# A 90-degree rotation of 96 images on one core: the first 1 MB load is made as two transfers of 4 KB pieces

## The chip, the cores and the metric

The kernel runs on one core of one Trainium2 chip. The metric is the device time of one execution in microseconds (us), taken as the median over several runs; lower is better. In what follows 1 MB of a load or store means 1024 KB, as the program counts it; rates in GB/s are in units of 10^9 bytes.

## The reference

Ninety-six images of 256 x 256 float32 values (a batch of 32 with 3 channels) are each turned by a quarter. Nothing is calculated on the values: every output value is an input value at another place.

```python
def setup_inputs():
    batch, c, h, w = 32, 3, 256, 256
    return {"x": np.random.randn(batch, c, h, w).astype(np.float32)}

def reference(x: np.ndarray) -> np.ndarray:
    return np.rot90(x, k=-1, axes=(-2, -1)).astype(np.float32)
```

25.17 million bytes have to be read from HBM and as many written.

## The kernel before

The input is seen as 24,576 rows of 256 values (1 KB each). They are cut into four groups, with the sizes 2, 2, 4 and 4 in units of 128 x 16 rows, that is 4, 4, 8 and 8 MB. Each group has its own tile in SBUF, `u0` to `u3` (`groups`, lines 41 to 44; the profile leaves the number out and shows `u`), and no tile is used twice, so that no load ever waits for space. Within a tile the rotation is done in place, by VectorE (DVE), which transposes blocks and reverses their order (`turn`, line 84), and by ScalarE (ACT), which copies pieces that had to step aside (`copy`, line 87). Spare room for these pieces is in two PSUM tiles (`spare0`, `spare1`) and two SBUF tiles (`extra`, `most`). The order of the DVE and ACT instructions is the order in which they are written; `keep` (line 75) fixes it.

**Loads.** All transfers are issued by the sync engine (SP), on one queue, in the order of the program. There are 15 loads. Group 0 is loaded in three of them: line 58, run twice, loads the two halves of slot 0 (`home[0]`), each 1 MB in 128 pieces (one for each partition) of 8 KB, and line 59 loads slot 1 (`home[1]`) with 2 MB, in 256 pieces of 8 KB. A piece of 8 KB is eight rows that lie side by side in HBM, and the 128 pieces of one load of line 58 lie side by side as well. Groups 1 to 3 are loaded by line 71 with 2 MB at a time, but the last 2 MB of group 3 are split in three (lines 67, 68 and 69: 0.5, 0.5 and 1 MB).

**Work.** The first DVE instruction (`turn_slab(u[:, 0], spare)`) reads both halves of slot 0, so it waits for both loads of line 58. Group 0 and group 1 follow as they land. The first instruction on group 2 reads pieces of all four of its loads, and from there DVE goes through groups 2 and 3.

**Stores.** There are ten, all behind the loads on the same SP queue. The first (line 178) waits in addition for the load of line 67 (`mark`), so that stores start when only the last 1.5 MB of loads are still under way. Groups 1 and 2 are stored by line 194, and group 3 by lines 190, 191, 192 and 194. Line 190 stores 64 pieces of 6 KB, line 191 stores 3 MB as soon as DVE and ACT are done with group 3, line 192 stores 64 pieces of 10 KB, and line 194 the last 4 MB.

**Semaphores of the transfers.** The transfers take eight semaphores in turn. So the issue of the ninth transfer, and of each one after it, has a wait for the transfer eight places before it, if that wait isn't already implied.

Of the kernel before, what the change touches and what calls it, by code (L numbers as in the profile page):

```python
# [9 lines left out]
def kernel(  # L10
# [14 lines left out]
    nc = tc.nc  # L25
# [6 lines left out]
    Q = E // 2  # L32
# [18 lines left out]
    def rows_of(rows, n):  # L51
        return rows[first[n] * P * R : (first[n] + sizes[n]) * P * R]


    ld = rows_of(rows_in, 0).rearrange("(s i p r) w -> s i p (r w)", s=2, i=2, p=P)
    home = [groups[0][:, s].rearrange("p (i f) -> p i f", i=2) for s in range(2)]
    for i in range(2):
        nc.sync.dma_start(out=home[0][:, i], in_=ld[1, i])  # L58
    nc.sync.dma_start(out=home[1], in_=ld[0].transpose([1, 0, 2]))  # L59
    for n in range(1, len(sizes)):  # L60
        I = sizes[n]
        ld = rows_of(rows_in, n).rearrange("(a i m r) w -> i m a (r w)", a=2, i=I, m=P // I)
# [162 lines left out]
```

## Time and profile before

| | us |
|---|---|
| median of 3 runs | 122.66 (122.62 to 122.70) |
| the profiled execution's own time | 122.64 |
| its span, first to last instruction | 120.8 |
| DVE busy, 25 instructions | 86.5 |
| ACT busy, 20 instructions | 29.0 |
| stores and loads together, 25 transfers | 97.6% of 16 DMA engines' span |

The time is 1.84 us more than the span; this part lies around the profiled instructions. The profile shows a transfer in two ways. Its issue is an instruction of the sync engine's sequencer (SPq), with a start and a duration. Its data move later, as packets on 16 DMA engines; a count of packets includes one very small packet for each transfer and engine, which tells the semaphore that this engine's part is done (25 transfers x 16 = 400 of them). "DMA share" in a table of windows is the time of the packets that start in the window, over 16 engines and the window's length; in short windows it can be over 1, since a packet counts where it starts.

### The profile page before, as it was taken

The page shows a single profiled execution, that of the slowest core. Times are in us where ns is not written, and L with a number is a line of the kernel's source. Part 1 is how long each engine was busy: PE and PEld are TensorE (multiplying, and loading weights), DVE is VectorE, ACT ScalarE, POOL GpSimd, SP SyncE. Part 2 cuts the span into 40 slices and gives each one's busy share as a digit, 9 for nine tenths or more (in the row PEclk, how much of TensorE's full clock was granted, in tenths as well). Part 3 has the DMA queues.
Part 4 walks back from the last instruction along what each step waited for, and adds up shares of the span by engine and source line. Part 5 has one row for each costly group of instructions (what it writes and reads, how often), then busy time and mean ns, then how long its engine had stood idle before and what let it go on. Part 6 is the DMA issues. An engine that isn't in the chain of part 4 may idle for free.

```text
span 120.8 us, 137 instructions
## 1 busy us (share of the span) xinstructions
DVE 86.5 (72%) x25; ACT 29.0 (24%) x20; POOL 0.2 (0%) x4
## 2 busy tenths in 40 slices
DVE  0039999999994099999999999999999990000000
ACT  0000400380005199508552296000003210000000
POOL 0000000000000000000000000000000000000000
DMA  2999999998989898989999999999999999999994
GB/s 87 431 434 423 447 434 434 434 521 347 521 347 521 347 521 347 510 358 412 456 407 418 423 428 434 418 434 434 423 434 434 434 434 456 401 423 456 434 434 174
DMA packets 3312, 50.33 MB, mean 417 GB/s; under 512 B 400, under 2 KB 400, under 8 KB 464
## 3 DMA queue, kind: packets, MB, share of 16 engines
q1 hardware_dynamic: 3312, 50.33, 97.6%
HBM read 25.17 MB, written 25.17 MB: 416 GB/s over the span
## 4 chain that ended last, share of the span: by engine, by line
DVE 44%; DMA 30%; SPq 4%; issue 3%; DVEq 0%
DVE u L84 34%; DMA u<-in_x_dram 30%; DVE spare L84 6%; DVE most L84 3%; SPq L71 3%; DVE extra L84 2%; SPq L58 1%; SPq L59 0%; DVEq L84 0%
## 5 line engine op out<-in xcount | busy, mean ns | idle before, releaser
L84 DVE STREAM_TRANSPOSE u<-u 128x2048 f32<-128x2048 f32 x16 | 59.6, 3792 | 0.3
L84 DVE STREAM_TRANSPOSE spare<-u 128x2048 f32<-128x2048 f32 (+1 forms) x4 | 11.8, 2982 | 12.6 <-DMA u<-in_x_dram 12.6
L87 ACT COPY u<-spare 128x512 f32<-128x512 f32 (+2 forms) x8 | 10.3, 1332 | 18.5 <-DVE u L84 13.7
L87 ACT COPY u<-extra 128x1024 f32<-128x1024 f32 (+1 forms) x3 | 5.7, 1938 | 11.1 <-DVE u L84 11.1
L87 ACT COPY u<-most 128x448 f32<-128x448 f32 x4 | 2.1, 563 | 20.4 <-DVE u L84 20.4
L87 ACT COPY spare<-u 128x1024 f32<-128x1024 f32 (+1 forms) x3 | 5.7, 1893 | 2.7 <-DMA u<-in_x_dram 2.7
L87 ACT COPY extra<-u 128x2048 f32<-128x2048 f32 x1 | 4.2, 4237 | 2.5 <-issue 2.5
L87 ACT ACT_TABLE_LOAD x1 | 1.3, 1283 | 13.0 <-DMA u<-in_x_dram 13.0
L84 DVE STREAM_TRANSPOSE extra<-u 128x2048 f32<-128x2048 f32 x1 | 3.9, 3898 | 0.0
L84 DVE STREAM_TRANSPOSE u<-spare 128x2048 f32<-128x2048 f32 x1 | 3.6, 3608 | 0.0
L84 DVE STREAM_TRANSPOSE most<-u 128x1792 f32<-128x1792 f32 x1 | 3.6, 3584 | 0.0
L84 DVE STREAM_TRANSPOSE spare<-spare 128x2048 f32<-128x2048 f32 x1 | 2.3, 2336 | 0.0
L84 DVE STREAM_TRANSPOSE extra<-extra 128x2048 f32<-128x2048 f32 x1 | 2.3, 2311 | 0.0
L209 POOL MEMSET const-uint8-127<- 128x1 uint8 x1 | 0.1, 102 | 0.0
L209 POOL MEMSET const-bfloat16-1.0<- 128x1 bf16 x1 | 0.1, 101 | 0.0
L209 POOL MEMSET const-float32-0.0<- 128x1 f32 x1 | 0.1, 98 | 0.2 <-issue 0.2
L209 POOL MEMSET const-float32-1.0<- 128x1 f32 x1 | 0.1, 98 | 0.0
## 6 DMA issues: line engine op xcount, KB each, us to landing
u<-in_x_dram SPq DMA_DIRECT2D x10, 2048.0 KB, 30.3
out_dram<-u SPq DMA_DIRECT2D x3, 4096.0 KB, 19.2
out_dram<-u SPq DMA_DIRECT2D x4, 2048.0 KB, 14.6
u<-in_x_dram SPq DMA_DIRECT2D x3, 1024.0 KB, 6.8
out_dram<-u SPq DMA_DIRECT2D x1, 3072.0 KB, 9.2
u<-in_x_dram SPq DMA_DIRECT2D x2, 512.0 KB, 33.4
out_dram<-u SPq DMA_DIRECT2D x1, 640.0 KB, 10.1
out_dram<-u SPq DMA_DIRECT2D x1, 384.0 KB, 5.6
```

Of the source, the lines that this page charges most:

```text
L58: nc.sync.dma_start(out=home[0][:, i], in_=ld[1, i])
L71: nc.sync.dma_start(out=to[i::I], in_=ld[i])
L84: keep(nc.vector.transpose(out=out, in_=in_))
L87: keep(nc.scalar.copy(out=out, in_=in_))
L209: nc = _bacc.Bacc("TRN2", target_bir_lowering=False, num_devices=1)
```

## The change

The first load of line 58, 1 MB in 128 pieces of 8 KB, becomes two transfers. Each covers all 128 partitions; the first moves the first 4 KB of each piece of 8 KB and the second the other 4 KB. Within one of these transfers the 4 KB pieces lie 8 KB apart in HBM. The second load of line 58 is unchanged, and so is all that follows, but all line numbers behind it grow by two.

```diff
-    for i in range(2):
-        nc.sync.dma_start(out=home[0][:, i], in_=ld[1, i])
+    tip = Q // 2
+    for f in (slice(0, tip), slice(tip, Q)):
+        nc.sync.dma_start(out=home[0][:, 0, f], in_=ld[1, 0][:, f])
+    nc.sync.dma_start(out=home[0][:, 1], in_=ld[1, 1])
     nc.sync.dma_start(out=home[1], in_=ld[0].transpose([1, 0, 2]))
```

`Q` is 2048 values, so `tip` is 1024 values, or 4 KB. In the program as it is built there are then 26 transfers, 16 of them loads. The semaphores are still taken in turn, so each transfer behind the first has the semaphore after the one that it had. For the waits of SP this comes to: the third load of group 2, which waited for no semaphore, now waits for the first 4 KB transfer; the fourth, which waited for the 1 MB transfer, waits for the second 4 KB transfer; every later load and every store waits for the same transfers as before. The first DVE instruction waits for three transfers in place of two. The instructions of DVE, ACT and GpSimd and their order are the same.

## The prediction

> **What bounds the kernel now.** I read the page first, for the share of each resource. DVE is busy for 72% of the span and ACT for 24%; the transfers are the resource that hardly ever rests.
>
> ```profile
> span 120.8 us, 137 instructions
> DMA  2999999998989898989999999999999999999994
> DMA packets 3312, 50.33 MB, mean 417 GB/s; under 512 B 400, under 2 KB 400, under 8 KB 464
> q1 hardware_dynamic: 3312, 50.33, 97.6%
> ```
>
> One digit is 3.02 us. The DMA row is full from the second slice to the last but one, and 97.6% of the span is 117.9 us, which is the stretch from the first packet to the last. So the end is the start of the data, plus the time of all packets, and idle time in between is near nothing. The change touches the first slice (the 2) and the number of packets.
>
> Second, the chain that ended last, in order of time, for how the start reaches the end (lines are left out):
>
> ```profile
> 0.73 0.37 SPq L58
> ...
> 1.16 0.42 SPq L58
> ...
> 5.53 36.61 DMA u<-in_x_dram
> ...
> 42.22 4.23 DVE spare L84
> ...
> 95.80 3.61 DVE u L84
> ```
>
> The loads stream until the fourth load of group 2 lands at 42.14; from there DVE works without a pause to 99.41, and line 191's store is issued at 99.47. What shifts the stream at its head shifts the landing at 42.14 by the same amount, and so DVE's chain too.
>
> Third, windows, for the head of the stream and for the place where both chains meet again. Columns: window and its length, busy time of DVE, ACT and GpSimd, clock, DMA share, GB/s.
>
> ```profile
> 1.00:1.70 0.70, 0.00 (x0) 0.00 (x0) 0.00 (x0) 1.00 0.00 0
> 1.70:2.50 0.80, 0.00 (x0) 0.00 (x0) 0.00 (x0) 1.00 0.73 164
> 2.50:2.70 0.20, 0.00 (x0) 0.00 (x0) 0.00 (x0) 1.00 0.00 0
> 1.70:4.85 3.15, 0.00 (x0) 0.00 (x0) 0.00 (x0) 1.00 0.87 333
> 4.85:7.25 2.40, 0.00 (x0) 0.00 (x0) 0.00 (x0) 1.00 1.03 434
> 99.85:100.70 0.85, 0.00 (x0) 0.00 (x0) 0.00 (x0) 1.00 0.99 412
> 100.70:101.00 0.30, 0.00 (x0) 0.00 (x0) 0.00 (x0) 1.00 2.17 915
> 101.00:101.35 0.35, 0.00 (x0) 0.00 (x0) 0.00 (x0) 1.00 0.00 0
> ```
>
> The first MB (128 packets, 1.70 to 4.85) takes 3.15 us and the second some 2.42. The difference, 0.73 us, I call the ramp: 16 first packets start between 1.70 and 2.50, one for each engine, then none until 2.70, so each first packet lasts long (0.73 x 0.80 us = 0.59 us on average). After 4.85 there is no second ramp, though another transfer begins there. At the other end, the packets of line 191 start together between 100.70 and 101.00 (915 GB/s is 16 packets of 16 KB, one for each engine, and two of 6 KB, then none): the queue had just run empty when this store came. So DVE's chain and the transfers are both at the limit there, and an edit would have to move both. One at the head does.
>
> Fourth, packet prices, from windows whose packets have one size: 7.8 to 9.8 (8 KB), 23 to 26 (32 KB) and 99.85 to 100.70 (6 KB, with 12 tiny ones).
>
> ```profile
> DMA packets 101, 0.83 MB, mean 414 GB/s; under 512 B 0, under 2 KB 0, under 8 KB 0
> q1 hardware_dynamic: 101, 0.83, 97.7%
> ...
> DMA packets 48, 1.57 MB, mean 524 GB/s; under 512 B 0, under 2 KB 0, under 8 KB 0
> q1 hardware_dynamic: 48, 1.57, 121.6%
> ...
> DMA packets 69, 0.35 MB, mean 412 GB/s; under 512 B 12, under 2 KB 12, under 8 KB 69
> q1 hardware_dynamic: 69, 0.35, 98.9%
> ```
>
> Share x 16 x window / packets gives 0.977 x 16 x 2.0 / 101 = 0.3095 us for 8 KB, 1.216 us for 32 KB, and 0.236 us for 6 KB (0.989 x 16 x 0.85 / 57, the tiny ones counted as nothing). Between 8 and 32 KB a KB costs 0.0378 us; that leaves 0.007 us per packet that doesn't depend on size. The same line gives 0.234 for 6 KB, so the measured 6 KB packet is within 0.002 us of it.
>
> **The change, step by step.**
>
> *Packets.* Of the first MB, each engine had 8 packets of 8 KB; it gets 16 of 4 KB. No 4 KB packet is in the trace. From below it can't cost less than half of 8 KB, 0.155 us (sum +0). From above I take the 6 KB packet, 0.236 us: 16 x 0.236 - 8 x 0.3095 = +1.30 us. The line gives 0.158, and the 6 KB row lies on that line, so I take 0.158: 16 x 0.158 - 8 x 0.3095 = +0.05 us. One more tiny packet per engine is at most the 0.002 x 57 / 12 = 0.01 us by which the 6 KB window is over the line. Together +0.06 us on every engine, and as no engine rests before 100.7, nothing hides it.
>
> The Trainium skill, "DMA: Bandwidth & Descriptors", in the warning on iDMA beside HBM reads, tabulates a load stream with 4 KiB rows alone at 408.7 GB/s. By it the first MB would need 2.57 us where the second now takes 2.42, and the sum would be +0.15 in place of +0.06 us; the trace has no such stream to compare.
>
> *Issue.* SP gets one more issue. The two of line 58 took 0.37 and 0.42 us, the one of line 59 with 256 pieces 0.43; the new ones have 128 pieces, so 0.4 us each, and 0.05 between. Only the first issue lies on the path, and it begins at 0.73 as before; from the spread of these rows its length may differ by 0.06 us either way. I take 0. All issues behind it come 0.45 us later. They are covered by data already queued: before, the second transfer was issued at 1.16 and its data began at 4.85. Now the first transfer alone holds 8 x 0.158 = 1.3 us of work behind its ramp, until about 3.6; the second transfer's packets, by the first's delay from issue to last start (0.73 to 2.50, 1.8 us), are there by about 2.95. Cover 0.65 us; without it, the shortfall would be paid one to one.
>
> *Waits on SP.* The third load of group 2 now waits for the first 4 KB transfer. Its turn comes at 4.88 + 0.45 = 5.3; that transfer's data end near 3.8 and land, with the 0.55 us by which the first MB landed behind its last packets (0.73 + 4.7 = 5.43 against 4.85 to 4.90), at 4.35. The wait is 0. The fourth load waits for the second 4 KB transfer, which lands near 5.5; its turn is at 5.9, where it waited before until 5.48. In both cases what stands behind on SP is later loads, with 8 MB and more queued ahead, some 20 us of cover. The other waits, those of all stores among them, are for the same transfers, and move with the stream.
>
> *DVE and ACT.* The first DVE instruction needs the second MB, which lands 0.06 later; DVE rests again for 4.53 us before 42.22, so this is lost in that gap. Landing at 42.14, DVE's end and line 191 all move by +0.06. So do the 16 engines.
>
> *The ramp.* 0.73 us at the head, and the only place where halving a piece could gain. If it all went: -0.73. If it were paid a second time by the second transfer: +0.73. The 16 engines each start one first packet between 1.70 and 2.50 and all start a second between 2.70 and 3.00; engines that began 0.7 us apart end together, so they wait for something that doesn't depend on how long each one's packet is. I take 0.
>
> Sum: +0.05 + 0.01 + 0 + 0 = +0.06, on the execution's own 122.64: 122.70 us. The median of the runs is 0.02 above that execution, so I forecast 122.72.
>
> **Rivals.**
>
> *The ramp shrinks (faster).* If a first packet's long time goes with its size, the first round is over sooner and the stream runs at full rate earlier. For it: the first packets last 0.59 us where later ones take 0.31, and they are the ones that get smaller. Against it: they end together whatever their start. If half the ramp goes: -0.37 + 0.06 = -0.31, 122.35 us. DVE's chain, hung on 42.14, would give it all on. The Trainium skill, "Perfetto Trace Analysis", under DMA optimizations, says that splitting may let some transfers start sooner, if the engines are generally idle; here they are idle only at the head, which this trace shows.
>
> *4 KB reads are slower than the line (slower).* Place: the 256 data packets of the first MB, read 8 KB apart. For it: nothing under 8 KB is ever loaded in this trace; the 6 KB row is a store. Against it: that row is on the line. Halfway between the two, 0.197 us a packet, the sum is 16 x 0.197 - 8 x 0.3095 + 0.01 = +0.69: 123.35 us. It decides (over 0.245 us) from 0.169 us a packet.
>
> *The ramp is paid twice (slower).* If the second transfer, now close behind, starts up on its own: +0.73 + 0.06, 123.45 us. Against it: no ramp at 4.85, where a transfer follows another. The Trainium skill, "DMA: Bandwidth & Descriptors", under rules for kernel authors, asks for 1 MiB or more per transfer, and its anatomy of a transfer gives a fixed cost of about 2.0 us (for transfers issued by GpSimd); taken as not overlapped that would be 124.7 us, and the seam at 4.85 disagrees.
>
> *It does nothing for the reader.* No instruction waits for a half alone: DVE waits for all three transfers. So an earlier half has no taker, and this rival ends where the forecast does.
>
> **How the numbers follow.** What a measurement of this kernel can tell from no change is about 0.2%, 0.245 us. The forecast has 0.50, with a range of its own of 122.55 to 122.90; the shrinking ramp 0.20 (122.1 to 122.4); slow 4 KB reads 0.20 (122.95 to 124.0); the second ramp 0.10. The forecast lies wholly within 0.2%, so the chances are 0.20, 0.50 and 0.30. The range 122.30 to 123.30 leaves out about 0.06 below and 0.14 above.
>
> **What would show it.** In the changed profile: packets go up by 128 + 16 to 3456; windows of 4 KB packets alone give 0.158 us each; the first MB ends 3.2 us after its first packet, with first packets still starting near 1.7; the wait at 42.14 ends at about 42.2 and line 191 is issued at about 99.53. A first round that is over before 2.7 would show the first rival, over 0.169 us per packet the second, and a stretch without packets near 3.6 the third. The forecast is wrong if the load of group 2 lands more than 0.2 us off 42.2, or if DVE's stretch of 57.3 us from there changes its length.

## The result and the profile after

The changed kernel takes 123.43 us (median of 6 runs, 123.40 to 124.08) against 122.64 for the kernel before (6 runs, 122.62 to 122.70). It is slower by 0.79 us. The ratio over all runs is 1.0073, with a 95% interval of 1.0059 to 1.0087; the two medians alone give 1.0064. The profiled execution took 123.48 us with a span of 121.7.

The page of the changed kernel, the rows that answer to those of before:

```profile
span 121.7 us, 138 instructions
DMA  3999999999999999999999999999999999999994
DMA packets 3456, 50.33 MB, mean 414 GB/s; under 512 B 416, under 2 KB 416, under 8 KB 736
q1 hardware_dynamic: 3456, 50.33, 97.4%
```

The packets are those that were counted beforehand, 128 + 16 more. The engines are nearly as full as before (97.4%). Summed over the trace, the packets take 118.5 us of an engine's time on average, where they took 118.0. So 0.5 of the 0.9 us of span is in the packets; the rest is time in which some engines wait, as shown below.

The chain that ended last, in order of time (start, length, what):

```profile
0.73 0.37 SPq L59
...
1.16 5.25 DMA u<-in_x_dram
...
6.42 36.66 DMA u<-in_x_dram
...
43.26 4.10 DVE spare L86
...
96.32 3.60 DVE u L86
```

The second 4 KB transfer lands at 6.41, where 5.5 was expected, and the fourth load of group 2 at 6.42 + 36.66 = 43.08 in place of 42.14: +0.94. The whole loss is there before DVE's long stretch begins.

Windows of the changed kernel's head (window, length, busy of DVE, ACT and GpSimd, clock, DMA share, GB/s), in the first four lines those of before, then two that separate the two 4 KB transfers:

```profile
1.70:2.50 0.80, 0.00 (x0) 0.00 (x0) 0.00 (x0) 1.00 0.69 189
2.50:2.70 0.20, 0.00 (x0) 0.00 (x0) 0.00 (x0) 1.00 0.91 307
1.70:4.85 3.15, 0.00 (x0) 0.00 (x0) 0.00 (x0) 1.00 0.87 263
4.85:7.25 2.40, 0.00 (x0) 0.00 (x0) 0.00 (x0) 1.00 1.01 420
...
2.50:3.90 1.40, 0.00 (x0) 0.00 (x0) 0.00 (x0) 1.00 0.93 231
4.43:5.15 0.72, 0.00 (x0) 0.00 (x0) 0.00 (x0) 1.00 0.97 398
```

and the kernel before in those last two:

```profile
2.50:3.90 1.40, 0.00 (x0) 0.00 (x0) 0.00 (x0) 1.00 0.89 374
4.43:5.15 0.72, 0.00 (x0) 0.00 (x0) 0.00 (x0) 1.00 0.99 410
```

From 2.50 to 3.90, when the engines work on the first 4 KB transfer, they are busy but get 231 GB/s in place of 374. From 4.43 to 5.15, all in the second transfer, they are near the rate of before. Over 1.70 to 4.85 the changed kernel is behind by (333 - 263) x 3.15 = 0.22 MB, 0.5 us at 434 GB/s. The packets of 1.70 to 3.90 and of 4.43 to 5.15 give the price of a 4 KB packet in each transfer:

```profile
DMA packets 116, 0.48 MB, mean 216 GB/s; under 512 B 0, under 2 KB 0, under 8 KB 116
q1 hardware_dynamic: 116, 0.48, 84.5%
...
DMA packets 70, 0.29 MB, mean 398 GB/s; under 512 B 0, under 2 KB 0, under 8 KB 70
q1 hardware_dynamic: 70, 0.29, 96.6%
```

0.845 x 16 x 2.2 / 116 = 0.256 us in the first transfer, 0.966 x 16 x 0.72 / 70 = 0.159 us in the second. Packets of the same size, from the two halves of the same 8 KB stretches of memory, cost 0.256 us and then 0.159. The 0.256 is a mean of unlike packets: in the trace's records of single packets, 45 of the 116 took 0.16 us, as all packets of 4.43 to 5.15 did, and 62 took from 0.20 to 0.64 us. So not every packet is dearer; more than half of them are held up.

The 0.5 us are a mean over the engines; the loss that counts is that of the last one. The tiny packets ("under 512 B") show where each engine ends a transfer. For the second MB, the kernel before has all 16 of them in 7.30 to 7.60:

```profile
DMA packets 32, 0.13 MB, mean 437 GB/s; under 512 B 16, under 2 KB 16, under 8 KB 16
```

and the changed kernel 14 in 7.60 to 8.30 and the last two in 8.30 to 8.57:

```profile
DMA packets 53, 0.32 MB, mean 456 GB/s; under 512 B 14, under 2 KB 14, under 8 KB 14
...
DMA packets 15, 0.11 MB, mean 394 GB/s; under 512 B 2, under 2 KB 2, under 8 KB 2
```

Engines that ended a transfer within 0.3 us of each other now do so within 0.97 us, and the last is about 1.0 us later than the last of before (DVE, which waits for it, starts at 9.04 where it started at 8.05). A load has landed when its last engine is done, so group 2 is late by 0.94 and not by 0.5. The delay isn't evened out on the way: by the times of the tiny packets, the engines' spread is between 0.92 and 0.96 us in every transfer from the second MB to line 192's store. At the end, DVE gives 0.4 us back: its stretch from the landing to the issue of line 193's store is 43.08 to 99.99, 56.9 us, where it was 57.3, since the first transpose took 4.10 in place of 4.23 and two later ones 7.16 in place of 7.55. It doesn't help the last engine, which still has work when this store comes:

```profile
100.70:101.00 0.30, 0.00 (x0) 0.00 (x0) 0.00 (x0) 1.00 0.89 369
101.00:101.35 0.35, 0.00 (x0) 0.00 (x0) 0.00 (x0) 1.00 1.35 568
```

Before, all engines began on this store together and then showed no start for 0.35 us; now they come to it one after another. The tiny packets that end line 192's store (100.93 to 101.89; one of the 17 belongs to the store ahead of it) and line 193's (108.64 to 109.20) show what the spread becomes:

```profile
DMA packets 62, 0.51 MB, mean 533 GB/s; under 512 B 17, under 2 KB 17, under 8 KB 39
...
DMA packets 42, 0.27 MB, mean 476 GB/s; under 512 B 16, under 2 KB 16, under 8 KB 16
```

It falls from 0.93 to 0.52 us. So the engines that came early ran empty and waited for line 193's store, which is issued 0.52 us later than before, and the last engine didn't. Its delay is what the end keeps: the last tiny packet of the program starts at 120.44, where it was 119.64. The trace doesn't name the engines; that one and the same engine is last from the head to the end is inferred from the spread.

### The profile page after: what moved, and what is told of

It is laid out like the page before. It is cut to its first block, busy times and chain, and to the rows that moved or that the text cites. A ratio compares the mean times of both kernels' runs of the same rounds, so it can differ in the third digit from the quotient of the medians.

```text
span 121.7 us, 138 instructions
## 1 busy us (share of the span) xinstructions
DVE 86.0 (71%) x25; ACT 28.5 (23%) x20; POOL 0.2 (0%) x4
## 3 DMA queue, kind: packets, MB, share of 16 engines
q1 hardware_dynamic: 3456, 50.33, 97.4%
## 4 chain that ended last, share of the span: by engine, by line
DVE 44%; DMA 34%; issue 3%; SPq 0%; DVEq 0%
DMA u<-in_x_dram 34%; DVE u L86 33%; DVE spare L86 5%; DVE most L86 3%; DVE extra L86 2%; SPq L59 0%; DVEq L86 0%
```

## The experiments

All but f4 are edits of the changed kernel, in the lines that load the first MB (some also those behind it); f4 loads group 0 as the kernel before does. The diffs are cut to the lines that matter, and some loop headers are left out. Times are medians, with the kernel before between 122.65 and 122.79 in the same sets of runs.

### Head, pitch or length of the transfer

**e1_second.** The first MB whole, the second in halves:

```diff
-        nc.sync.dma_start(out=home[0][:, 0, f], in_=ld[1, 0][:, f])
-    nc.sync.dma_start(out=home[0][:, 1], in_=ld[1, 1])
+        nc.sync.dma_start(out=home[0][:, 1, f], in_=ld[1, 1][:, f])
```
(with the whole first MB loaded ahead of the loop)

> The first MB is whole again (128 pieces of 8 KB), and the second MB is loaded by two transfers of 4 KB pieces in its place. Theory A (pieces of 4 KB are slow only while the stream starts up, in its first 2 to 3 us): 122.7 us, the sum of the prediction, +0.06. Theory B (4 KB pieces that lie 8 KB apart are slow wherever they are read): about 123.4, as in the changed kernel. Theory C (one transfer more, or a short one, ahead of the stream is what costs): 122.7, as the first transfer is 1 MB long again.

Measured: 123.64 us, 1.0067 (1.0052 to 1.0082). Its head is that of the kernel before, and the first 4 KB transfer, now seen in 5.25 to 6.50, is slow all the same; the second, in 7.32 to 7.76, is not:

```profile
1.70:4.85 3.15, 0.00 (x0) 0.00 (x0) 0.00 (x0) 1.00 0.92 333
5.25:6.50 1.25, 0.00 (x0) 0.00 (x0) 0.00 (x0) 1.00 0.91 279
7.32:7.76 0.44, 0.00 (x0) 0.00 (x0) 0.00 (x0) 1.00 1.02 419
```

So it isn't the start of the stream, and it isn't a short transfer ahead of it: theories A and C fall. B comes nearest in time, but the second transfer, with pieces 8 KB apart too, runs at full rate, so B as it was put doesn't hold either.

**e2_dense.** The same two transfers with pieces side by side:

```diff
+    dense = rows_of(rows_in, 0).rearrange("(s i f p r) w -> s i f p (r w)", s=2, i=2, f=2, p=P)
-        nc.sync.dma_start(out=home[0][:, 0, f], in_=ld[1, 0][:, f])
+        nc.sync.dma_start(out=home[0][:, 0, f], in_=dense[1, 0, h])
```

> As the changed kernel, with two first transfers of 128 pieces of 4 KB, but the pieces of each lie side by side in HBM (0.5 MB in one stretch); the values land in other places of slot 0, so the part of the output that comes from this MB is not the rotation. Theory A (small pieces at the head): 123.4. Theory B (pitch of 8 KB): 122.7. Theory C (short first transfer): 123.4.

Measured: 122.99 us, 1.0031 (1.0003 to 1.0058), but 10 runs spread from 122.53 to 123.99. In the profiled execution (122.84) the engines get 403 GB/s from 2.60 to 4.60 in packets of 4 KB, so the slow stretch is gone with the holes. The places in SBUF that are written are the same as in the changed kernel, which leaves the side of HBM. What spreads the runs wasn't found, and there is no trace of one of the slower ones.

**e3_parts.** Halves by partitions, with 8 KB pieces:

```diff
-        nc.sync.dma_start(out=home[0][:, 0, f], in_=ld[1, 0][:, f])
+        nc.sync.dma_start(out=home[0][j::2, 0], in_=ld[1, 0][j::2])
```

> The first MB is loaded by two transfers of 0.5 MB, but by every second partition, 64 pieces of 8 KB in each. Theory A (small pieces at the head): 122.7 or less, as no piece is under 8 KB. Theory B (holes of a piece's length between the pieces): about 123.4, if holes of 8 KB count as those of 4 KB do. Theory C (short first transfer): 123.4.

Measured: 123.91 us, 1.0089 (1.0065 to 1.0113), and for another reason. The first issue takes 0.59 us in place of 0.37, only 82 GB/s start in 1.70 to 2.50 and 205 in 2.50 to 3.30; from 3.50 to 5.00 the rate is 410. So the start is late: the 16 tiny packets that end the first MB lie in 5.15 to 5.60, where they lay in 4.85 to 5.15. That is some 0.45 us of the 1.2. The rest comes in the second MB, which is loaded as before: its last ones lie in 7.70 to 8.70, where they lay in 7.30 to 7.60, and why is open. Holes of 8 KB between pieces of 8 KB show no slow stretch.

**e4_cross.** Two transfers of 1 MB, 256 pieces of 4 KB each:

```diff
-        nc.sync.dma_start(out=home[0][:, 0, f], in_=ld[1, 0][:, f])
-    nc.sync.dma_start(out=home[0][:, 1], in_=ld[1, 1])
+        nc.sync.dma_start(out=home[0][:, :, f], in_=ld[1].transpose([1, 0, 2])[:, :, f])
```

> The first two MB are loaded by two transfers of 1 MB, as in the kernel before, but each takes 4 KB of each of the 256 pieces of 8 KB; the number of transfers is that of the kernel before. Theory A (small pieces at the head): 123.4 or somewhat more, since the pieces stay small for 2 MB. Theory B (pitch): 124.2, twice the loss. Theory C (short first transfer): 122.75.

Measured: 124.86 us, 1.0166 (1.0151 to 1.0181): 240 GB/s from 2.50 to 6.00, then 420 from 7.30 to 8.50. The slow stretch is over twice as long and the loss 2.1 us; the number of transfers is that of before. Theory C falls; A and B both expected less.

### Small pieces, the size of the hole

**f1_pair_rev.** 4 KB pieces without holes, in one transfer:

```diff
-        nc.sync.dma_start(out=home[0][:, 0, f], in_=ld[1, 0][:, f])
+    cut2 = lambda t: t.rearrange("p (t f) -> p t f", t=2)[:, ::-1]
+    nc.sync.dma_start(out=cut2(home[0][:, 0]), in_=cut2(ld[1, 0]))
```

> The first MB is one transfer again, but of 256 pieces of 4 KB: for each partition first the upper and then the lower half of its 8 KB. So there are pieces of 4 KB at the head, and no hole, since both halves of a stretch of 8 KB are read one after the other. Theory D (what costs is the first read in each aligned stretch of 8 KB: the stream opens no more than about 61 such stretches per us, as in the run with the crossing halves, and a later read in an open stretch runs at full rate): no loss by this, 122.7 with the 0.06 for more packets; less by up to 0.25 if the start is as early as in the run with pieces side by side. Rival S (small packets at the head as such): 123.4.

Measured: 123.20 us, 1.0045 (1.0030 to 1.0060). No theory gave this time; the windows say why:

```profile
1.70:2.50 0.80, 0.00 (x0) 0.00 (x0) 0.00 (x0) 1.00 0.84 72
2.50:3.50 1.00, 0.00 (x0) 0.00 (x0) 0.00 (x0) 1.00 0.51 164
3.50:5.20 1.70, 0.00 (x0) 0.00 (x0) 0.00 (x0) 1.00 1.03 424
```

The issue of this form takes 0.73 us in place of 0.37, and the data start some 0.5 us late, which is the loss. From 3.50 the 4 KB packets run at 424 GB/s. So 4 KB packets as such aren't slow when both halves are read together; rival S falls by the windows, not by the time.

**f2_quarter.** The cut at 2 KB:

```diff
-    tip = Q // 2
+    tip = Q // 4
```

> The changed kernel with the cut at 2 KB: first transfer 128 pieces of 2 KB, second 128 pieces of 6 KB, of the same 8 KB. Theory D: the first pass takes 128 / 61 = 2.1 us though it moves only 0.25 MB, the second 0.75 x 2.44 = 1.85 us: 3.95 in place of 2.45 for the MB, +1.5, 124.15 us. Rival P (a piece of 4 KB with a hole behind it costs a fixed excess of time, 0.9 us in all, whatever its size): 123.5. Rival R (the loss goes with the bytes that are read beside holes, here half as many): 123.1.

Measured: 123.31 us, 1.0060 (1.0039 to 1.0082), nearest to rivals R and P (123.1 and 123.5), not theory D. In 2.50 to 3.20 the rate is 260 GB/s (some engines have gone on to the second transfer by then), in 4.00 to 4.70 it is 413.

**f3_mixed.** Four transfers, lower and upper halves crossed:

```diff
+    for i, f in ((0, slice(0, tip)), (1, slice(tip, Q)), (0, slice(tip, Q)), (1, slice(0, tip))):
+        nc.sync.dma_start(out=home[0][:, i, f], in_=ld[1, i][:, f])
```

> The first two MB in four transfers of 0.5 MB, all of 4 KB pieces 8 KB apart: lower halves of the first MB, upper halves of the second, upper halves of the first, lower halves of the second. Theory D: the first two transfers are slow (256 stretches opened, 4.2 us in place of 2.45), the last two at full rate; about +1.8 to +2.2, 124.5 to 124.9. Rival L (the lower halves are the slow ones, wherever they stand): the first and the fourth are slow, the second and third are not; the time is about the same, the windows tell it.

Measured: 124.67 us, 1.0165 (1.0150 to 1.0180). One window inside each transfer:

```profile
2.50:3.65 1.15, 0.00 (x0) 0.00 (x0) 0.00 (x0) 1.00 0.99 232
4.35:4.95 0.60, 0.00 (x0) 0.00 (x0) 0.00 (x0) 1.00 0.98 403
5.95:7.00 1.05, 0.00 (x0) 0.00 (x0) 0.00 (x0) 1.00 0.82 211
8.30:9.00 0.70, 0.00 (x0) 0.00 (x0) 0.00 (x0) 1.00 1.13 468
```

Slow, full, slow, full. (The last window also holds 8 KB packets of the load behind; its 4 KB packets all took 0.16 us, while of those in the third window 8 in 55 did.) The time is theory D's, but the second transfer reads stretches that nothing had touched and is not slow, while the third reads touched ones and is: D falls. So does L, since the fourth (lower halves) is at full rate and the third (upper) is slow. The time alone would have confirmed a wrong theory.

**f4_wide.** The first load of group 1 in two transfers of 8 KB pieces, 16 KB apart, and the first two MB as before:

```diff
-                nc.sync.dma_start(out=to[i::I], in_=ld[i])
+                for f in (slice(0, E // 2), slice(E // 2, E)) if (n, i) == (1, 0) else (slice(None),):
+                    nc.sync.dma_start(out=to[i::I][:, :, f], in_=ld[i][:, :, f])
```

> The first two MB as in the kernel before; the first load of group 1 (128 pieces of 16 KB) is cut into two transfers, each with 8 KB of every 16 KB. Theory D (the unit is 8 KB): no slow pass, 122.7 to 122.75. Rival W (any hole costs: the stream covers no more than about 500 GB/s of addresses, holes counted): the first of the two takes 2 MB / 500 GB/s = 4.2 us in place of 2.45, +1.7, 124.4 us.

Measured: 122.80 us, 1.0007 (0.9997 to 1.0016), with 423 GB/s inside the first of the two transfers (12.70 to 14.60) and 438 inside the second (14.70 to 17.00). So holes between 8 KB pieces cost nothing here; W falls.

**g2_pitch12** and **g3_pitch16.** The changed kernel with pieces of 4 KB at other distances (g3 with `t=4` over 16 rows a partition):

```diff
+    far = rows_of(rows_in, 0)[16 * P : 28 * P].rearrange("(p t r) w -> t p (r w)", t=3, r=4)
-        nc.sync.dma_start(out=home[0][:, 0, f], in_=ld[1, 0][:, f])
+        nc.sync.dma_start(out=home[0][:, 0, f], in_=far[h])
```

> As the changed kernel, but the two transfers of 128 pieces of 4 KB read pieces 12 KB apart (holes of 8 KB), so that neighbouring partitions alternate between lower and upper halves of the 8 KB stretches; slot 0 gets other values, so that part of the output isn't the rotation. Theory H (a transfer whose pieces are all lower halves, or all upper, gets only about 250 GB/s, half of what the memory gives to both): no slow transfer, 122.7. Rival G (any hole beside pieces of 4 KB): 123.4 or more.

> The same with pieces 16 KB apart: the first transfer reads the first 4 KB of each 16 KB, the second the next 4 KB. Theory H: all lower halves, then all upper, as in the changed kernel: 123.4. Rival G: 123.4 or more. If only a quarter of the memory serves the pieces of one transfer, the first one takes twice as long again, some 125.

Measured: 122.97 us, 1.0022 (1.0012 to 1.0031), at 12 KB; 123.47 us, 1.0070 (1.0053 to 1.0087), at 16 KB. At 16 KB the first transfer gets 225 GB/s from 2.30 to 3.90 and the second 399 from 4.75, as at 8 KB. At 12 KB, with larger holes than at 8, the rate is at full height by 3.90:

```profile
1.70:2.50 0.80, 0.00 (x0) 0.00 (x0) 0.00 (x0) 1.00 0.51 87
2.50:3.90 1.40, 0.00 (x0) 0.00 (x0) 0.00 (x0) 1.00 0.86 301
3.90:5.00 1.10, 0.00 (x0) 0.00 (x0) 0.00 (x0) 1.00 1.02 417
```

What remains of the loss (0.28 us, clear of noise) goes with a slower first 1 to 2 us. So the distance decides, 8 or 16 KB against 4 or 12: pieces that fall in both halves of the 8 KB stretches are fast, pieces that all fall in the same half are slow in the first such transfer. Theory H comes nearest in time (122.7 and 123.4); rival G fails at 12 KB. Why a second transfer, all in one half too, isn't slow, H doesn't say.

### Why some such transfers are slow and others not

**g1_order.** The four transfers of f3 in the order lower, lower, upper, upper:

```diff
+    for f in (slice(0, tip), slice(tip, Q)):
+        for i in range(2):
+            nc.sync.dma_start(out=home[0][:, i, f], in_=ld[1, i][:, f])
```

> The same four transfers of 4 KB pieces as in the run with mixed halves, in another order: lower halves of the first MB, lower of the second, upper of the first, upper of the second. Theory D (first read in a stretch of 8 KB) is out, as the second transfer of the mixed run was at full rate on untouched stretches. Theory O (a transfer is slow unless it reads the other half than the transfer ahead of it): slow, slow, full rate, slow; some 3 slow transfers of 0.9 us each, 125.3 us. Theory T (every second one of such transfers is at full rate, whatever it reads): slow, fast, slow, fast, 124.7 us. Theory E (as with crossing halves in two transfers of 1 MB): slow, slow, fast, fast, 124.9 us.

Measured: 124.62 us, 1.0156 (1.0139 to 1.0173): 245 GB/s through 2.50 to 6.00, both lower transfers, then 406 from 6.90 to 8.20, the third; in the fourth the 4 KB packets took 0.18 us on average, close to the full rate's 0.16. That is the order of theory E. O and T fall by the windows, though T's time (124.7) is the nearest.

**h1_upper**, **h2_apart**, **h3_again.** Upper halves first; the second MB between the two halves; the lower halves twice:

```diff
+    for f in (slice(tip, Q), slice(0, tip)):                              # h1
+    nc.sync.dma_start(out=home[0][:, 0, :tip], in_=ld[1, 0][:, :tip])     # h2
+    nc.sync.dma_start(out=home[0][:, 1], in_=ld[1, 1])
+    nc.sync.dma_start(out=home[0][:, 0, tip:], in_=ld[1, 0][:, tip:])
+        nc.sync.dma_start(out=home[0][:, 0, f], in_=ld[1, 0][:, :tip])    # h3
```

> The changed kernel with the two 4 KB transfers in the other order: upper halves first. If the lower halves are no different from the upper, the first transfer is slow again and the second at full rate: 123.4. If it is the lower halves that are slow (Rival L): the first is at full rate and the second slow, and about the same time.

> The same two transfers, but the whole second MB (8 KB pieces) is loaded between them: lower halves of the first MB, all of the second MB, upper halves of the first MB. Theory O (a transfer of halves is at full rate only right behind one of the opposite halves): both are slow, each by 0.8 to 0.9 us, 124.3. Theory V (what was read once near by makes the other half fast, however long ago): only the first is slow, 123.4.

> The lower halves of the first MB are loaded twice, into both halves of the place (so that part of the output isn't the rotation). Theory O: the second follows one of the same halves and is slow as well, 124.2. Theory V', the data or the rows of the memory are at hand after the first read: the second is at full rate, 123.4.

Measured: h1 123.48 us, 1.0066 (1.0048 to 1.0084), slow (257 GB/s from 2.50 to 3.90), then full (401 from 4.65): upper and lower don't differ. h2 124.01 us, 1.0108 (1.0083 to 1.0133): the first is slow (240), the last, a whole MB later, is not (406 from 6.70 to 7.85), so it needn't stand right behind the other. O falls by the rates, though its time (124.3) is nearer than that of V (123.4). The rest of the loss begins in the first transfer too: eight of its engines end it between 4.43, when the changed kernel's last was done, and 5.12. h3 124.07 us, 1.0119 (1.0099 to 1.0140): 272 GB/s from 2.50 to 5.50, over both transfers. The same bytes read a second time are slow again, so a first reading doesn't make a second one fast, and V' falls.

**i1_long.** All of group 0 in four transfers of 1 MB: lower halves of slot 0, of slot 1, upper halves of slot 0, of slot 1:

```diff
+    for f in (slice(0, tip), slice(tip, Q)):
+        for s in range(2):
+            nc.sync.dma_start(out=home[s][:, :, f], in_=ld[1 - s].transpose([1, 0, 2])[:, :, f])
```

> All 4 MB of group 0 by four transfers of 1 MB, each of 256 pieces of 4 KB: lower halves of 2 MB in two transfers, then the upper halves of the same 2 MB in two. Theory Q (the lower and the upper halves of the 8 KB stretches are served by separate parts of the memory, each with about 250 GB/s, and the engines read ahead by some 0.25 to 0.4 MB in all, 16 to 24 KB each; so the transfer behind a slow one starts with data already read): 4.2 us, 4.2 us, then some 2.5 to 3.2 us for the third, which lives on what was read ahead and on a wait that is over, and again 4.2 us for the fourth, as read-ahead covers no more; 15.3 to 15.9 us in place of 9.8, some 128.3 us. Rival Z (a transfer is at full rate whenever it makes up for halves that were read unevenly before, without limit): 4.2, 4.2, 2.5, 2.5, some 126.3 us.

Measured: 124.94 us, 1.0178 (1.0160 to 1.0196). Both theories fall, and clearly:

```profile
2.50:6.00 3.50, 0.00 (x0) 0.00 (x0) 0.00 (x0) 1.00 0.90 240
7.20:8.50 1.30, 0.00 (x0) 0.00 (x0) 0.00 (x0) 1.00 1.02 422
9.70:11.00 1.30, 0.00 (x0) 0.00 (x0) 0.00 (x0) 1.00 1.02 419
```

The second transfer reads lower halves alone, of new places, behind 1 MB of lower halves, and is at full rate. So one half of the stretches isn't limited to 250 GB/s at all, and the reason that theory H gave falls with Q.

**j1_four**, **j2_swap.** The same 4 MB in eight transfers of 0.5 MB (j1), and i1 with slot 1 ahead of slot 0 (j2):

```diff
+            for i in range(2):                                            # j1, in i1's loops
+                nc.sync.dma_start(out=home[s][:, i, f], in_=ld[1 - s, i][:, f])
+        for s in (1, 0):                                                  # j2
```

> Group 0's 4 MB by eight transfers of 128 pieces of 4 KB: the lower halves of its third, fourth, first and second MB (the order in which the kernel takes them), then the upper halves in the same order. Theory U (the slowness is a settling of the 16 engines at the head of such a stream, over after 1 MB of pieces of one half, whatever is read then): slow, slow, then six at full rate, 124.9 us, as the run with 2 MB of halves. Theory X (the first two MB of group 0 in memory are not affected and the last two are): the same order of slow and fast. Rival W (in this form, with 0.5 MB a transfer, every transfer of lower halves is slow): slow four times, then fast, 126.5 us.

> The run with 2 MB of halves (four transfers of 1 MB), but with slot 1, which lies in the first two MB of group 0, ahead of slot 0 in both passes. Theory U (settling at the head): the first transfer is slow again, the other three are at full rate, 124.9 us. Theory X (the place in memory decides): the first is at full rate and the second slow, if it is slow at all.

Measured: j1 124.79 us, 1.0174 (1.0159 to 1.0190):

```profile
2.50:6.00 3.50, 0.00 (x0) 0.00 (x0) 0.00 (x0) 1.00 0.91 241
6.50:8.20 1.70, 0.00 (x0) 0.00 (x0) 0.00 (x0) 1.00 1.03 419
8.90:13.30 4.40, 0.60 (x1) 0.00 (x0) 0.00 (x0) 1.00 1.03 421
```

Two transfers slow, six at full rate. j2: 240 GB/s from 2.50 to 6.00 and 410 from 7.45, the same with the other place at the head, so the place doesn't decide; X and W fall. Theory U has the rates, but not the time: that is 126.78 us (1.0326, 1.0309 to 1.0343) in place of 124.9, and 1.8 us more than i1 at the same rates: slot 0's upper halves now land last of the 4 MB, DVE starts at 15.50 where it started at 12.74 in i1, and its gap at 42 us, which was to cover a late start, is used up.

What these runs leave: at the head of a stream of 4 KB pieces that all lie in one half of the 8 KB stretches, the rate is some 210 to 280 GB/s; it is full as soon as the other half follows, and after 1 MB also for more of the same (j1, i1). One description fits every run: a transfer is slow while it takes what has been read of one half further ahead of the other than it was so far, up to 1 MB, and at full rate otherwise. (In f3 the third transfer is the first that takes the upper halves ahead.) This was formed after the runs, none was made to test it, and it names no cause. That it's a settling of the 16 engines against each other would fit the completions that spread from 0.3 to about 1 us; it was not shown, and f3's third transfer, slow although the two ahead of it had been read, speaks against a settling that happens once. Which part of HBM or of the engines makes the slow stretch stays open.

No version that beats the kernel before came out of these runs.

## Why the prediction was wrong

The forecast was 122.72 us, within 0.2% of before, in a range to 123.30; it came out at 123.43. By its own steps:

**Packets, the step that failed.** The prediction put a 4 KB packet at 0.158 us, on the line through the 8 and 32 KB rows, and took the 6 KB packets of a store as a sign that the line holds below 8 KB. For packets that nothing holds up the line is right: 0.159 us in the second 4 KB transfer. But the price was taken to depend on size alone. In the first transfer a packet took 0.256 us on average, beyond even the upper end that was set by the 6 KB row (0.236). That this goes with where the pieces lie in HBM, all in one half of the 8 KB stretches, is shown by f1, e2 and g2: with 4 KB packets that don't lie so, the rate is over 400 GB/s from 3.50, 2.60 and 3.90 on. Why such pieces are slow, and why only at first, stays open. No row of the trace before could show it: its only pieces under 8 KB are written, not read.

**The same step, the sum over engines.** +0.06 us was set "on every engine". The mean loss was about 0.5 us and the last engine's about 1.0. What sets the end is the last engine, and its delay goes through to the end, where 0.79 us remained.

**Issue and ramp.** First issue 0.37 us at 0.73, first packets from 1.70, no stretch without packets near 3.6: as forecast. The ramp did change: 189 GB/s and 307 in the first windows where there were 164 and 0, so small first packets do get the stream going earlier, as the first rival said. The reason for setting the ramp at 0, that the engines' first packets end together however long they are, didn't hold: 37 packets start in 1.70 to 2.50, where there were 16. The slow stretch behind takes more back than this gains.

**Waits.** The loads and stores wait for what was forecast. The second 4 KB transfer landed at 6.41, not 5.5, so the fourth load of group 2 was issued at 6.42, 0.5 us later than thought, with many MB ahead of it on the queue: no effect.

**DVE and the end.** That a delay at the head passes through to 42.14 whole held (+0.94). That DVE's stretch keeps its length didn't: it was 0.4 us shorter, but the last engine had become the bound. So both signs came that the prediction had named for being wrong.

**The rivals.** The second, 4 KB reads slower than the line, had 123.35 us with a chance of 0.20 and came close. Its mark of 0.169 us a packet was passed (0.256 in one transfer and 0.159 in the other, some 0.2 over both). Its place was half right: the first 128 packets, not all 256. That its time came so near is luck in part: the 0.197 was taken halfway between two bounds, and it set the same loss on every engine, where the end came from the last one. The third, a second ramp, gave 123.45 us, nearest of all, by a cause that wasn't there: no stretch without packets shows near 3.6. The stream of 4 KiB rows at 408.7 GB/s in the Trainium skill ("DMA: Bandwidth & Descriptors", the warning on iDMA beside HBM reads) agrees with the second transfer's 398 and with e2's 403. The estimate from it was +0.15 us; like the line, it says nothing of the distance between the pieces.

## What to carry to other kernels

When a load is cut so that each transfer takes a part of every row, look at where its pieces lie in HBM, not only at their size and number: in this kernel 4 KB pieces 8 or 16 KB apart were read at some 210 to 280 GB/s for up to 1 MB, and pieces of 4 KB side by side, or 8 KB pieces 16 KB apart, at over 400. And where the engines are busy to the end, judge an edit at the head by the engine that comes out of it last: here the spread of 0.95 us at the end of the first MB was still 0.93 at 101 us.

## What the runs showed that was not expected

- Later transfers of the same pieces run at full rate once 1 MB has been read slowly (j1: 241 GB/s, then 419), even with lower halves of places not read before.
- The form of the first transfer sets the start of the data. 128 pieces of 8 KB are issued in 0.37 us; 64 pieces of 8 KB take 0.59 (e3), and 256 pieces of 4 KB in f1's order 0.73, and in both only 72 to 82 GB/s start from 1.70 to 2.50, where it was 164. It isn't the number of pieces alone: i1's first transfer, 256 pieces of 4 KB in another order, is issued in 0.43 us. So a smaller or finer first transfer isn't always an earlier one.
